# A two-layer decoder trunk on one core: first transfers on two queues, the last block in one half, tiles in multiples of 64 bytes

## The chip, the core and the metric

The kernel runs on one core of a Trainium2 chip. The core has a matrix engine (TensorE, PE in the profile; its weight loads are listed apart as PEld), a vector engine (VectorE, DVE), an engine for functions of single elements (ScalarE, ACT), GpSimd (POOL) and SyncE (SP), and 16 DMA engines that move data between memory (HBM) and the core's on-chip memory (SBUF). A transfer is issued by SP or by ACT and goes into that issuer's queue. TensorE writes its sums into PSUM, from which VectorE and ScalarE read them.

The metric is the device time of one execution in microseconds. Three runs of the kernel before took 2359.57 to 2361.82 us, median 2360.89.

## The reference

The input x has 256 tokens of 2048 features, in float32. Two layers follow one another; each is a mixer and a gated MLP, both with a root-mean-square norm before them and the input added after them.

```python
for l in range(DEPTH):                      # DEPTH = 2
    h = rms_norm(x, mix_norm[l])
    if l % 2 == 0:
        h = mixer_ab(h, ...)                # one input projection, gated MLP over tokens and
                                            # a gated linear recurrence, one output projection
    else:
        h = mixer_c(h, ...)                 # attention with a forget gate, 16 heads of 128
    x = x + h
    h = rms_norm(x, ffn_norm[l])
    x = x + conv_ffn(h, ...)                # up (2048 -> 2 x 5632), conv of width 3, silu gate, down
return x
```

Nearly all of the arithmetic is products of 256 tokens with weight matrices in float32, about 430 MB of weights in all, each read once.

## The kernel before

All arrays are laid out feature-major: a tile has 128 features on the partitions and 256 tokens in a row. x stays in SBUF as 16 such tiles (xT), in seven buffers of 1, 1, 2, 2, 2, 4 and 4 tiles (x0, x1, x2, x4, x6, x8, x12 by their first tile). Each float32 number is split into a high part, rounded to the type that TensorE multiplies in one pass (fp32r), and the rest, the low part. A product is formed as high x high + high x low + low x high.

For weights this is done by `weights` (L130): a transfer into w by SP (L137), the high part wh by ScalarE (L139), the low part wl by VectorE (L141). There are four buffers for w and three each for wh and wl. For inputs it is done by `split` (L199), with the norm's gain multiplied in: high part by ScalarE (L204), low part by VectorE (L205); `feed_split` (L230) applies it to one tile of x, and the result, tile a, holds high and low part side by side, 2 x 256 columns. The norm's factor per token is applied after the product.

`project` (L144) makes one block of 128 output features: for each of 16 feature tiles one matmul of 512 columns (wh against both parts of a, L155) and one of 256 (wl against the high part, added to the second half, L158). Its result has two halves, which `fold` (L187) or `add_x` (L262) adds: ScalarE copies the second half to SBUF (L265), VectorE adds the first half to x (L266) and then the copy (L267). `project_tok` (L163) makes 512 output features for all tokens at once, with the tokens' parts as the weights that are loaded into TensorE: per feature tile two halves of the tokens with three matmuls of 512 columns each (L180 to L182).

The first work of the kernel is `project_tok` on w_v with feed=True. Its loop takes one feature tile at a time for the first four and two at a time after that; before each step it issues the x transfers that FETCH lists for that k, calls feed_split for its tiles, lets one step of waiting side work run (`tick`), and calls weights. Transfers of x tiles from 8 on are issued by ACT, the others by SP, ahead of the weights of the same step. Fifteen matmuls on a tile of ones (warm) run before. The order in which each engine gets its instructions is fixed by a scheduler when the program is built; an engine works through its list in that order and waits where a tile isn't ready. A transfer signals on one of a few semaphores, in turn; one that gets a semaphore still in use waits until the earlier transfer has landed.

The side work in the first blocks is the sum of squares for the norm (`feed_square`, L237 to L241). At the end of the second MLP, `down` computes the last four blocks with project, and `finish_x` stores each x tile as it is done.

Tiles are given SBUF addresses one behind the other in pools, in steps of 32 bytes. Several tiles are only 1, 2, 24 or a few columns wide, so the tiles behind them stand at addresses that are a multiple of 32 but not of 64.

Of the kernel before, what the change touches and what calls it, by code (L numbers as in the profile page):

```python
# [14 lines left out]
P = 128  # L15
# [9 lines left out]
WARM = 15  # L25
FETCH = {0: (0,), 1: (1, 2, 8), 2: (4, 6), 3: (12,)}
# [19 lines left out]
def tile_trunk(ctx: ExitStack, tc: tile.TileContext, x, pp_d, cst_d, mlev_d, msk_d,  # L46
# [13 lines left out]
    def nm(base):  # L60
        count[0] += 1
        return f"{base}_{count[0]}"
# [13 lines left out]
    nc.sync.dma_start(pp[:, 0:C_FFN], pp_d[:, 0:C_FFN])  # L76
# [53 lines left out]
    def weights(src, n, rows=None):  # L130
# [5 lines left out]
        w = pool.tile([P, n], F32, tag="w", name=nm("w"), bufs=nw)  # L136
        nc.sync.dma_start(w if rows is None else w.rearrange("p (m c) -> p m c", m=rows), src)  # L137
        wh = pool.tile([P, n], F32R, tag="wh", name=nm("wh"), bufs=ns)
        SC.activation(wh, w, AF.Copy)  # L139
        wl = pool.tile([P, n], F32R, tag="wl", name=nm("wl"), bufs=ns)  # L140
        V.tensor_tensor(wl, w, wh.bitcast(F32), ALU.subtract)  # L141
        return wh, wl

    def project(wsrc, acts, chunks=(8, 8), k0=0, run=2):  # L144
        ps = pm.tile([P, 512], F32, tag="pm", name=nm("pm"))
        nk = sum(chunks)
        done = 0
        for c in chunks:
            lo = (k0 + done) * P
            tick()  # L150
            wh, wl = weights(wsrc[:, lo:lo + c * P], c * P)
            for k1 in range(0, c, run):
                ks = range(k1, min(k1 + run, c))
                for k in ks:
                    PE.matmul(ps, wh[:, k * P:(k + 1) * P], acts[done + k],  # L155
                              start=done + k == 0, stop=False, skip_group_check=True)
                for k in ks:
                    PE.matmul(ps[:, S:2 * S], wl[:, k * P:(k + 1) * P], acts[done + k][:, 0:S],  # L158
                              start=False, stop=done + k == nk - 1, skip_group_check=True)
            done += c  # L160
        return ps

    def project_tok(wsrc, norm, feed=False):  # L163
        ps = [pm.tile([P, 512], F32, tag="pm", name=nm("pm")) for _ in range(2)]
        k = 0
        for c in ((1, 1, 1, 1) + (2,) * 6 if feed else (2,) * 8):
            if feed:
                for c0 in FETCH.get(k, ()):
                    t, c0, n = fetch[c0]
                    (SC if c0 >= 8 else nc.sync).dma_start(t, x[:, c0:c0 + n, :])  # L170
                for i in range(c):
                    norm.feed_split(k + i)
            tick()
            wh, wl = weights(wsrc[:, k * 512:(k + c) * 512], c * 512)
            for T in range(2):
                for i in range(c):
                    a = norm.a[k + i]
                    ah, al = a[:, T * P:(T + 1) * P], a[:, S + T * P:S + (T + 1) * P]
                    h, l = (t[:, i * 512:(i + 1) * 512] for t in (wh, wl))
                    PE.matmul(ps[T], ah, h, start=k + i == 0, stop=False)  # L180
                    PE.matmul(ps[T], ah, l, start=False, stop=False)  # L181
# [17 lines left out]
    def split(dst, src, gain=None):  # L199
# [3 lines left out]
        else:  # L203
            SC.activation(dst[:, 0:S], src, AF.Copy, scale=gain)  # L204
# [3 lines left out]
    def rsq(dst, src, n):  # L208
        tag = "sq" if dst.shape[-1] == S else f"rm{len(dst.shape)}{dst.shape[-1]}"
        m = tp.tile(list(dst.shape), F32, tag=tag, name=nm("rm"))  # L210
        t = tp.tile(list(dst.shape), F32, tag=tag, name=nm("rt"))
# [11 lines left out]
    class Norm:  # L223
# [6 lines left out]
        def feed_split(self, k):  # L230
            a = apool.tile([P, 512], F32R, tag="a", name=nm("a"), bufs=KT)
            split(a, xT[k], pp[:, self.col + k:self.col + k + 1])
            self.a[k] = a
# [14 lines left out]
        def finish(self, tok=False):  # L248
# [10 lines left out]
            Rt = cp.tile([P, 2], F32, tag="Rt", name=nm("Rt"), bufs=2)  # L259
# [10 lines left out]
    def mixer_ab(norm):  # L270
# [90 lines left out]
        ge = hp.tile([P, 3 * NH], F32, tag="ge", name="ge")  # L361
# [32 lines left out]
        def hgrn(h):  # L394
# [15 lines left out]
            for li in reversed(range(NL)):  # L410
# [8 lines left out]
                if li:  # L419
                    V.tensor_tensor(odd, odd, view(tot, m, (-m, 2), (2, m // 2), (0, n)), ALU.mult)  # L420
                    nt = hp.tile([P, m], F32, tag=f"tot{n}", name=nm("tot"), bufs=1)
# [34 lines left out]
            so = hp.tile([P, 2], F32, tag="so", name=nm("so"), bufs=2)  # L456
# [74 lines left out]
    def mixer_c(norm):  # L531
# [9 lines left out]
        gq = hp.tile([P, 1], F32, tag="gq", name="gq")  # L541
# [23 lines left out]
        def attend(h, q, k, v):  # L565
# [20 lines left out]
            mxs = hp.tile([P, 2], F32, tag="mxs", name=nm("mxs"), bufs=2)  # L586
            sms = hp.tile([P, 2], F32, tag="sms", name=nm("sms"), bufs=2)
# [62 lines left out]
    def ffn(l, norm, last):  # L650
# [52 lines left out]
        def down(g, hid):  # L703
            final = g == HT // GRP - 1
            late = []
            for q in range(4):
                if final and q == 3:
                    for m in range(4 * q, KT):
                        ps = project(w_dn[l, m], hid, chunks=(6, 5), k0=g * GRP, run=2)
# [3 lines left out]
                        add_x(m, ps)  # L713
# [124 lines left out]
```

## Time and profile before

| | |
|---|---|
| median of three runs | 2360.89 us (2359.57 to 2361.82) |
| the profiled execution | 2359.05 us |
| its span, first to last instruction | 2357.2 us |
| granted TensorE clock, mean over the span | 1.000 |
| moved by DMA | 439.56 MB, 186 GB/s over the span |

The page gives the busy time of each engine and its share of the span, then the chain of work that ended last, followed back from the last instruction. Groups and timelines have lines of the form: start and length, engine, line of the kernel, operation, tiles written and read, shapes, count; in brackets stands how long the engine was idle before, and what ended that. Windows give the busy time of each engine (with its number of instructions), the granted clock, the DMA engines' share and GB/s for a stretch of time. DMA issues stand with the time from issue to landing. SPq and ACTq are the queues' issuing instructions. Matmuls overlap, so a row's length is longer than the distance to the next one's start.

### The profile page before, as it was taken

The numbers are of one execution on the slowest core, as the hardware profiler recorded it, in microseconds if no ns is written. First come the engines' busy times: TensorE is split into PE (matmuls) and PEld (weight loads), VectorE is DVE, ScalarE is ACT, GpSimd is POOL, SyncE is SP. The second block draws the span as 40 slices with busy tenths as digits, with TensorE's granted clock in tenths as the row PEclk, the third lists the DMA queues.
The fourth block names the chain that finished last, engine by engine and source line by source line (L and its number), as shares of the span: only waits on it lengthen the run. The fifth ranks groups of instructions, "written<-read, shape, count | busy, mean of one in ns | idle before, by whom it ended". The sixth has DMA issues, their size and how long they took to land.

```text
span 2357.2 us, 33532 instructions
## 1 busy us (share of the span) xinstructions
PE 2348.7 (100%) x12528; PEld 2011.1 (85%) x12528; DVE 1689.0 (72%) x2760; ACT 1286.3 (55%) x2085; POOL 0.2 (0%) x4
## 2 busy tenths in 40 slices
PE   9999999999999999999999999999999999999999
PEld 7888888888888888888888888888888888888887
DVE  7777877878847757866766666777878757758755
ACT  7655665655545545544555455556555545545533
POOL 0000000000000000000000000000000000000000
PEclk9999999999999999999999999999999999999999
DMA  7544455655555565555655554556555565565563
GB/s 269 179 166 150 150 197 206 222 188 188 179 196 196 184 192 197 184 181 164 202 171 180 171 161 169 188 188 239 190 190 189 179 203 190 179 202 191 178 193 117
DMA packets 194740, 439.56 MB, mean 186 GB/s; under 512 B 14208, under 2 KB 108688, under 8 KB 194448
## 3 DMA queue, kind: packets, MB, share of 16 engines
q1 hardware_dynamic: 193424, 434.20, 55.3%
q10 hardware_dynamic: 1152, 3.21, 0.4%
q8 instruction: 98, 1.61, 0.3%
q14 instruction: 66, 0.54, 0.1%
HBM read 435.24 MB, written 2.11 MB: 186 GB/s over the span
## 4 chain that ended last, share of the span: by engine, by line
PE 99%; DMA 0%; ACT 0%; DVE 0%; SPq 0%; issue 0%; ACTq 0%
PE pm L155 42%; PE pm L158 21%; PE pm L728 6%; PE pm L727 6%; PE pm L729 6%; PE pm L181 5%; PE pm L182 5%; PE pm L180 5%; PE px L432 1%; DMA w<-in_w_v 0%; PE px L606 0%; PE px L692 0%; PE px L570 0%; PE px L577 0%; PE px L601 0%; PE px L402 0%
## 5 line engine op out<-in xcount | busy, mean ns | idle before, releaser
L141 DVE TENSOR_TENSOR wl<-w,wh 128x1024 fp32r<-128x1024 f32 (+1 forms) x840 | 1004.3, 1196 | 556.2 <-ACT wh L139 553.9
L139 ACT ACTIVATE wh<-w 128x1024 fp32r<-128x1024 f32 (+1 forms) x840 | 871.1, 1038 | 962.2 <-PE pm L155 473.1
L155 PE MATMUL pm<-a,wh 128*128 128x512 f32 x3600 | 1135.3, 396 | 0.0
L158 PEld LDWEIGHTS pm<-a,wl 128*128 128x128 f32 x3600 | 676.1, 188 | 158.9
L158 PE MATMUL pm<-a,wl 128*128 128x256 f32 x3600 | 708.7, 278 | 0.0
L155 PEld LDWEIGHTS pm<-a,wh 128*128 128x128 f32 x3600 | 549.6, 189 | 1.5 <-DVE a L205 0.8
L727 PE MATMUL pm<-wh,hid 128*128 128x512 f32 x660 | 257.1, 390 | 0.0
L728 PE MATMUL pm<-wl,hid 128*128 128x512 f32 x660 | 256.8, 389 | 0.0
L729 PE MATMUL pm<-wh,hid 128*128 128x512 f32 x660 | 256.8, 389 | 0.0
L180 PE MATMUL pm<-wh,a 128*128 128x512 f32 x512 | 203.1, 398 | 2.6 <-ACT wh L139 2.6
L181 PE MATMUL pm<-wl,a 128*128 128x512 f32 x512 | 200.8, 392 | 0.6 <-DVE wl L141 0.6
L182 PE MATMUL pm<-wh,a 128*128 128x512 f32 x512 | 200.2, 391 | 0.0
L729 PEld LDWEIGHTS pm<-wh,hid 128*128 128x128 f32 x660 | 123.9, 188 | 25.7
L727 PEld LDWEIGHTS pm<-wh,hid 128*128 128x128 f32 x660 | 123.9, 188 | 25.5
L728 PEld LDWEIGHTS pm<-wl,hid 128*128 128x128 f32 x660 | 123.9, 188 | 25.3
L180 PEld LDWEIGHTS pm<-wh,a 128*128 128x128 f32 x512 | 96.2, 188 | 22.4 <-ACT wh L139 3.7
L181 PEld LDWEIGHTS pm<-wl,a 128*128 128x128 f32 x512 | 96.2, 188 | 21.3 <-DVE wl L141 2.2
L182 PEld LDWEIGHTS pm<-wh,a 128*128 128x128 f32 x512 | 96.1, 188 | 19.8
L667 ACT ACTIVATE conv<-ev,pp 128x256 f32<-128x256 f32 x176 | 102.9, 585 | 5.5 <-DVE ev L196 5.5
L189 DVE TENSOR_TENSOR ev<-pm,ev 128x256 f32<-128x256 f32 x225 | 93.9, 417 | 1.1 <-ACT ev L188 1.0
L669 DVE SCALAR_TENSOR_TENSOR conv<-ev,pp,conv 128x254 f32<-128x254 f32 x176 | 85.0, 483 | 6.2
L668 DVE SCALAR_TENSOR_TENSOR conv<-ev,pp,conv 128x255 f32<-128x255 f32 x176 | 84.1, 478 | 4.4 <-ACT conv L667 4.4
(185 smaller groups left out, 1644.3 us busy)
## 6 DMA issues: line engine op xcount, KB each, us to landing
w<-in_w_up SPq DMA_DIRECT2D x352, 512.0 KB, 4.2
w<-in_w_dn SPq DMA_DIRECT2D x150, 512.0 KB, 3.6
w<-in_w_cqkv SPq DMA_DIRECT2D x96, 512.0 KB, 3.5
w<-in_w_abo SPq DMA_DIRECT2D x32, 512.0 KB, 3.6
w<-in_w_cg SPq DMA_DIRECT2D x32, 512.0 KB, 3.6
w<-in_w_co SPq DMA_DIRECT2D x32, 512.0 KB, 3.6
w<-in_w_f SPq DMA_DIRECT2D x16, 512.0 KB, 3.7
w<-in_w_q SPq DMA_DIRECT2D x16, 512.0 KB, 3.6
```

The costliest lines, as they stand in the source:

```text
L139: SC.activation(wh, w, AF.Copy)
L141: V.tensor_tensor(wl, w, wh.bitcast(F32), ALU.subtract)
L155: PE.matmul(ps, wh[:, k * P:(k + 1) * P], acts[done + k], start=done + k == 0, stop=False, skip_group_check=True)
L158: PE.matmul(ps[:, S:2 * S], wl[:, k * P:(k + 1) * P], acts[done + k][:, 0:S], start=False, stop=done + k == nk - 1, skip_group_check=True)
L180: PE.matmul(ps[T], ah, h, start=k + i == 0, stop=False)
L181: PE.matmul(ps[T], ah, l, start=False, stop=False)
L182: PE.matmul(ps[T], al, h, start=False, stop=k + i == KT - 1)
L189: V.tensor_tensor(t, ps[:, 0:S], t, ALU.add)
L667: SC.activation(c, z, AF.Identity, bias=pp[:, cb:cb + 1], scale=w(2))
L727: PE.matmul(ps[T], ah, h, start=k + i == 0, stop=False)
L728: PE.matmul(ps[T], ah, lo_, start=False, stop=False)
L729: PE.matmul(ps[T], al, h, start=False, stop=k + i == GRP - 1)
```

## The change

Three things are changed.

The start: the first weights (256 KB) are issued by SP before anything else, the first five x buffers (x0 to x6) by ACT, in front of ScalarE's table load, and pp's first columns by SP after the weights. x8 and x12 are issued by SP, behind the weights of the steps k=4 and k=8 (an ordering without a wait keeps them there). The high part of the first x tile is made by VectorE. In the single-tile steps the six matmuls run with wh first, both halves and both parts, and then wl. There are 11 warm-up matmuls in place of 15.

The end: the last block is summed in one half of 256 columns with three matmuls of 256 columns per feature tile, and one VectorE addition to x replaces the copy and two additions.

The tiles: those that were 4 to 96 bytes wide, and pp (3216 bytes, now 3264), are rounded up to a multiple of 64 bytes (LANE is 16 numbers of 4 bytes), and only their first columns are used. The two helper tiles in `rsq` share one tag and size.

The core of the diff; the lines left out give the other small tiles (ge, tot, so, gq, mxs, sms) the same rounding as one1 and Rt:

```diff
-WARM = 15
-FETCH = {0: (0,), 1: (1, 2, 8), 2: (4, 6), 3: (12,)}
+WARM = 11
+FETCH = {4: (8,), 8: (12,)}
+LANE = 16
...
-    pp = cp.tile([P, NPP], F32, tag="pp", name="pp")
+    pp = cp.tile([P, -(-NPP // LANE) * LANE], F32, tag="pp", name="pp")
...
-    one1 = cp.tile([P, 1], F32, tag="one1", name="one1")
-
+    one1 = cp.tile([P, LANE], F32, tag="one1", name="one1")[:, 0:1]
+
+    first = wp.tile([P, 512], F32, tag="w", name=nm("w"), bufs=4)
+    nc.sync.dma_start(first, w_v[0, :, 0:512])
+    for t, c0, n in xload[:5]:
+        SC.dma_start(t, x[:, c0:c0 + n, :])
     nc.sync.dma_start(pp[:, 0:C_FFN], pp_d[:, 0:C_FFN])
...
+        if w is None:
+            w = pool.tile([P, n], F32, tag="w", name=nm("w"), bufs=nw)
+            deep["dma"] = nc.sync.dma_start(
+                w if rows is None else w.rearrange("p (m c) -> p m c", m=rows), src)
...
+                if narrow:
+                    for k in ks:
+                        for j, t in enumerate((wh, wh, wl)):
+                            o = S if j == 1 else 0
+                            PE.matmul(ps[:, 0:S], t[:, k * P:(k + 1) * P], acts[done + k][:, o:o + S],
+                                      start=done + k + j == 0, stop=j == 2 and done + k == nk - 1)
+                    continue
...
+            later = []
             if feed:
                 for c0 in FETCH.get(k, ()):
                     t, c0, n = fetch[c0]
-                    (SC if c0 >= 8 else nc.sync).dma_start(t, x[:, c0:c0 + n, :])
+                    later.append((t, c0, n))
                 for i in range(c):
-                    norm.feed_split(k + i)
+                    norm.feed_split(k + i, V if k == 0 else SC)
             tick()
-            wh, wl = weights(wsrc[:, k * 512:(k + c) * 512], c * 512)
+            wh, wl = weights(wsrc[:, k * 512:(k + c) * 512], c * 512, w=first if feed and k == 0 else None)
+            for t, c0, n in later:
+                r = nc.sync.dma_start(t, x[:, c0:c0 + n, :])
+                tc.add_manual_dep(r.ins, deep["dma"].ins.name, order, reason="queue order")
+            if feed and c == 1:
+                a = norm.a[k]
+                for j, (o, t) in enumerate(((0, wh), (S, wh), (0, wl))):
+                    for T in range(2):
+                        PE.matmul(ps[T], a[:, o + T * P:o + (T + 1) * P], t, start=k + j == 0, stop=False)
+                k += c
+                continue
...
-            Rt = cp.tile([P, 2], F32, tag="Rt", name=nm("Rt"), bufs=2)
+            Rt = cp.tile([P, LANE], F32, tag="Rt", name=nm("Rt"), bufs=2)[:, 0:2]
...
-                        ps = project(w_dn[l, m], hid, chunks=(6, 5), k0=g * GRP, run=2)
+                        ps = project(w_dn[l, m], hid, chunks=(6, 5), k0=g * GRP, run=2,
+                                     narrow=last and m == KT - 1)
...
-                        add_x(m, ps)
+                        if last and m == KT - 1:
+                            V.tensor_tensor(xT[m], xT[m], ps[:, 0:S], ALU.add)
+                        else:
+                            add_x(m, ps)
```

More of the change, by code (lines that the diff above doesn't have):

```diff
@@ L1 @@
+import math
 from contextlib import ExitStack
@@ L128, in tile_trunk, with weights @@
     deep = {"pool": None, "turn": 0}
-    def weights(src, n, rows=None):
+    def weights(src, n, rows=None, w=None):
         deep["turn"] += 1
@@ L209, in rsq @@
         tag = "sq" if dst.shape[-1] == S else f"rm{len(dst.shape)}{dst.shape[-1]}"
-        m = tp.tile(list(dst.shape), F32, tag=tag, name=nm("rm"))
-        t = tp.tile(list(dst.shape), F32, tag=tag, name=nm("rt"))
+        cols = dst.shape[-1] if dst.shape[-1] == S else LANE // math.prod(dst.shape[1:-1])
+        m, t = (tp.tile(list(dst.shape[:-1]) + [max(cols, dst.shape[-1])], F32, tag=tag, name=nm(n_))
+                [..., 0:dst.shape[-1]] for n_ in ("rm", "rt"))
         V.tensor_scalar(m, src, 1.0 / n, EPS, ALU.mult, ALU.add)
```

27 lines of the change are left out of this document (14 added, 13 removed).

## The prediction

> **What bounds the kernel.** The page's busy times and its chain of waits come first: is there one engine that everything waits for, and where does it not run?
>
> ```profile
> span 2357.2 us, 33532 instructions
> PE 2348.7 (100%) x12528; PEld 2011.1 (85%) x12528; DVE 1689.0 (72%) x2760; ACT 1286.3 (55%) x2085; POOL 0.2 (0%) x4
> PE 99%; DMA 0%; ACT 0%; DVE 0%; SPq 0%; issue 0%; ACTq 0%
> ```
>
> TensorE carries 99% of the chain, so only three things move the end: how long it idles before its stream closes up, the pace of the stream, and what follows its last matmul. Weight traffic, ScalarE and VectorE are covered by it everywhere else, and the change leaves all that order as it was from the second block of projections on. The timeline of the start:
>
> ```profile
> 0.72 1.28 ACT L119 ACT_TABLE_LOAD   x1 [0.72 <-PEq L827]
> 0.73 0.39 SPq L76 DMA_DIRECT2D pp<-in_pp  x1
> 0.76 0.39 ACTq L170 DMA_DIRECT2D x<-in_x  x1
> 1.04 5.10 PE L122 MATMUL warm<-ones 128*128 128x128 f32 x30 [1.04 <-DVE one L78]
> 1.17 0.42 SPq L170 DMA_DIRECT2D x<-in_x  x1
> 1.64 0.42 SPq L137 DMA_DIRECT2D w<-in_w_v  x1
> 5.72 0.51 ACT L204 ACTIVATE a<-x,pp 128x256 fp32r<-128x256 f32 x1 [3.72 <-DMA x<-in_x]
> 6.82 0.63 ACT L139 ACTIVATE wh<-w 128x512 fp32r<-128x512 f32 x1 [0.59 <-DMA w<-in_w_v]
> 7.50 0.73 PE L180 MATMUL pm<-wh,a 128*128 128x512 f32 x2 [1.36 <-ACT wh L139]
> ...
> 12.20 1.39 ACT L139 ACTIVATE wh<-w 128x512 fp32r<-128x512 f32 x2 [0.40 <-DMA w<-in_w_v]
> 13.49 1.29 ACT L204 ACTIVATE a<-x,pp 128x256 fp32r<-128x256 f32 x3
> 14.69 1.04 ACT L139 ACTIVATE wh<-w 128x1024 fp32r<-128x1024 f32 x1
> 15.64 0.90 ACT L204 ACTIVATE a<-x,pp 128x256 fp32r<-128x256 f32 x2
> 15.77 1.23 DVE L141 TENSOR_TENSOR wl<-w,wh 128x1024 fp32r<-128x1024 f32 x1 [0.27 <-ACT wh L139]
> 17.05 0.50 PE L181 MATMUL pm<-wl,a 128*128 128x512 f32 x1 [0.40 <-DVE wl L141]
> 21.03 0.40 ACT L237 ACTIVATE acc<-x 128x256 f32<-128x256 f32 x1
> 21.34 0.71 ACT L240 ACTIVATE sq<-x 128x256 f32<-128x256 f32 x2
> ```
>
> The first projection waits in turn for x, for the weights, for ScalarE's high part (wh) and for VectorE's low part (wl). From 17.05 us it runs without a gap, as the windows show:
>
> ```profile
> 2.00:4.00 2.00, 2.00 (x12) 2.00 (x11) 0.00 (x0) 0.01 (x1) 0.00 (x0) 1.00 0.85 275
> 8.00:11.00 3.00, 2.61 (x9) 1.43 (x9) 1.99 (x6) 2.08 (x5) 0.00 (x0) 1.00 1.01 387
> 17.05:33.00 15.95, 15.95 (x70) 13.21 (x71) 14.04 (x27) 13.53 (x24) 0.00 (x0) 1.00 0.85 281
> ```
>
> The columns after the length are PE, PEld, DVE, ACT, POOL, granted clock, DMA share and GB/s. The first block has 8 pairs of 12 matmuls, 96; 70 of them lie in the last row, 15.95 / 70 = 0.228 us each, so 26 were done at 17.05. A stream without any gap that ends at the same moment would have begun at 17.05 - 26 x 0.227 = 11.15 us. I call that the virtual start; only what the change does to this number counts at the start.
>
> **Part 1, the start.** The change issues the first weights (256 KB) first on SP, x0, x1 and x2-7 on ACT's queue beside them, puts x8-11 and x12-15 on SP behind the weights of k=4 and k=8, and computes the first high part of x on VectorE. The first x tile and weights no longer stand behind pp, x8-11 (512 KB, at 0.76) and each other. The issues, with their times to landing from 0 to 30 us:
>
> ```profile
> x<-in_x ACTq DMA_DIRECT2D x2, 512.0 KB, 5.3
> w<-in_w_v SPq DMA_DIRECT2D x4, 256.0 KB, 5.5
> x<-in_x SPq DMA_DIRECT2D x2, 128.0 KB, 4.8
> pp<-in_pp SPq DMA_DIRECT2D x1, 16.0 KB, 2.9
> ```
>
> x0 is now the first of its queue, as pp was, so 2.9 us is its lower bound and 4.8 its upper; I take 2.9, because pp too had one larger transfer beside it. x0 then lands at 0.76 + 2.9 = 3.7 us. A wait is added: the fifth x transfer (x6-7) reuses x0's semaphore, so it stands on ACT until x0 has landed, and the table load and the first wh are queued behind it; TensorE waits for that wh. So wh starts at 3.7 + 0.35 (an issue; the rows have 0.39) + 1.28 (table) = 5.35 us, where it started at 6.82. With 4.8 it would be 7.2 and nothing would be won there. VectorE makes the high part of x meanwhile, once pp, second on SP, has landed; its cover is 1.65 us of ScalarE.
>
> From there ScalarE sets the pace. In its new order, up to the weights of k=6,7, stand 4 wh of 512 columns at 0.645 (12.20 to 13.49 for two), 11 high parts of x at 0.43 (13.49 to 14.69 for three is 0.40 each, the pair at 15.64 0.45), one wh of 1024 at 0.95 (14.69 to 15.64), two squares at 0.31 and 0.35, a second wh at 1.04, and then, 0.05 us later, VectorE's wl at 1.23: 2.58 + 4.73 + 0.95 + 0.66 + 1.04 + 0.05 + 1.23 = 11.2 us. At that moment 38 matmuls can be done, 8.6 us of stream, and the 10 that are left, 2.3 us, cover the two squares, the wh and the wl of the next weights. The virtual start is 5.35 + 11.2 - 8.6 = 7.95 us, if the data are in time. The fourth weights are the tight ones: with them 4 x 256 KB of weights, 1 MB of x and pp must have landed, 2.1 MB. At the 275 to 387 GB/s of the rows from 1.7 us on that is 7.2 to 9.4 us; ScalarE asks for them after three wh and three high parts of x, at 5.35 + 1.94 + 1.29 = 8.6. I take 9.0, near the slow end since the queues start at the slow rate, so 0.4 us late: virtual start 8.35, gain 11.15 - 8.35 = **2.8 us** (bounds 0.9, with x0 after 4.8 us, and 3.2, with no late weights). Later weights (issued when VectorE frees a buffer at about 6.7) and x8-11 have 0.5 us or more to spare. Eleven warm-up matmuls for fifteen (5.10 us) end at about 4.8 us, before the first wh in either case, and the pause after them, 1.2 us to 6.0, is no longer than the 1.36 of now, in which the granted clock stayed at 1.00: nothing; should the pause cost clock, the stream still waits for ScalarE until 17 us.
>
> The page "DMA: Bandwidth & Descriptors" of the Trainium skill, under "Issuing engines are not separate DMA queues", says that transfers started from several engines run on the same 16 DMA engines and that a second issuer only saves the issuing time. The trace agrees so far as two queues together never pass 387 GB/s above. By that rule the second queue brings no bytes sooner, and what is won is the order alone; where the first four weights would be no earlier, rival C has the time.
>
> **Part 2, alignment.** Tiles of 4, 8 or 96 bytes per partition become multiples of 64, so what lies behind them moves from an odd multiple of 32 to a multiple of 64. Weight tiles, a, hid and yc were on 64 before and stay there. On TensorE's large matmuls that leaves the inputs ya and yb of the output projection of mixer AB, on 32 until now. The trace holds a pair for comparison: the same loop, the same 512 matmuls, once with ya and yb and once in mixer C with yc.
>
> ```profile
> 311.36:401.89 90.53, 90.53 (x514) 78.68 (x512) 63.58 (x97) 50.95 (x82) 0.00 (x0) 1.00 0.53 187
> 1529.23:1618.57 89.34, 89.34 (x514) 77.64 (x512) 62.83 (x96) 51.21 (x82) 0.00 (x0) 1.00 0.54 189
> ```
>
> The difference, 90.53 - 89.34 = **1.2 us**, is what the alignment is worth if it is the cause; the lower bound is 0, the upper 1.2 plus what the small matmuls give (rival E). The other tiles moved are read and written by VectorE and ScalarE, which the 99% covers.
>
> The page "SBUF — State Buffer" of the Trainium skill (its box on cachelines, under "Door 1: The DMA port swizzle") gives 16-byte lines. An offset of 32 bytes is a whole number of those, so by it the alignment would change nothing; the row of 90.53 speaks against it, not proof, and rival B has that case.
>
> **Part 3, the end.** The last block is summed in one 256-column half, so the copy of the second half and its addition go.
>
> ```profile
> 2349.29 0.62 PE L155 MATMUL pm<-hid,wh 128*128 128x512 f32 x2
> ...
> 2352.54 0.40 PE L158 MATMUL pm<-hid,wl 128*128 128x256 f32 x2
> ...
> 2353.00 0.28 PE L158 MATMUL pm<-hid,wl 128*128 128x256 f32 x1
> 2353.37 0.38 ACT L265 ACTIVATE ev<-pm 128x256 f32<-128x256 f32 x1 [3.50 <-PE pm L158]
> 2353.78 0.42 DVE L266 TENSOR_TENSOR x<-x,pm 128x256 f32<-128x256 f32 x1 [3.00 <-ACT ev L265]
> 2354.24 0.42 DVE L267 TENSOR_TENSOR x<-x,ev 128x256 f32<-128x256 f32 x1
> ```
>
> One addition can start at 2353.37 and end at 2353.79 instead of 2354.66: 0.87 us. On TensorE 11 matmuls of 512 and 11 of 256 columns become 33 of 256. The old ones took 2353.00 + 0.12 - 2349.29 = 3.83 us, the new ones 33 x 0.115 to 0.12 (0.40 - 0.28 between the starts of a pair) = 3.8 to 3.96; I take 0.05 dearer. Gain **0.8 us** (0.7 to 0.9). The store behind it keeps its 2.5 us to the end of the span.
>
> **The sum.** 2.8 + 1.2 + 0.8 = 4.8 us. The profiled execution took 2359.05 us (span 2357.2 and 1.85 around it), which becomes 2354.25. The median of the three runs is 1.84 us above it, so the forecast is 2360.89 - 4.8 = **2356.1 us**, 0.20% less, about at the edge of what a measurement of this kernel tells from no change (0.2%, 4.7 us).
>
> **Rivals.**
> A is the forecast. With its start anywhere from 2.0 to 3.2 and the end from 0.7 to 0.9 us it gives 2355.6 to 2357.0.
> B: the start and the end hold, the alignment brings nothing; 1.2 us less won, 2357.3. For it speaks that the two output projections sit in different stages with other work on VectorE (63.58 against 62.83 us); against it, that ScalarE was busier in the quicker one.
> C: the queues only share what there is. x2-7 on ACT take half of the DMA engines and the fourth weights land as late as before (ScalarE's 12.20 row shows the third and fourth landing about then), or x0 lands at 4.8 us. The start then gains 0 to 0.9, the sum is 2.0 to 2.9, 2358 to 2358.9.
> D, on the other side: new addresses slow the stream. All weights and inputs get other addresses, those of the first pools 128 bytes further on, and TensorE reads the two operands side by side. 4.8 / 12528 = 0.38 ns a matmul cancels the gain; 1 ns more each gives 2360.89 + 12.5 - 4.8 = 2368.6. Against it: weights and inputs in different buffers show one duration (a and yc),
>
> ```profile
> L155 PE MATMUL pm<-a,wh 128*128 128x512 f32 x3600 | 1135.3, 396 | 0.0
> L155 PE MATMUL pm<-yc,wh 128*128 128x512 f32 x256 | 80.5, 396 | 0.0
> L432 PE MATMUL px<-E 128*128 128x128 f32 x112 | 15.5, 279 | 0.0
> L692 PE MATMUL px<-cst,y 128*128 128x128 f32 x64 | 8.0, 272 | 0.0
> ```
>
> and the distance between weights and inputs in the first pools stays the same.
> E: alignment also helps the small matmuls, whose inputs E, pt, qk, kq and st stand on 32. E's take 279 ns, those of the aligned y 272, 2.5%; the windows give all matmuls into px 91.11 us,
>
> ```profile
> 0.00:2357.20 2357.20, 91.11 (x582) 76.57 (x582) 53.92 (x136) 33.02 (x106) 1.00 0.56 186
> ```
>
> so at most 2.3 us more, and with the aligned ones left out I take 1.6: 2354.5.
>
> **Chances.** A 0.58, of which six tenths lie beyond 4.7 us: its sum is just there, and the 0.4 us for late weights may not be owed; E 0.16; C 0.11; B 0.09; D 0.06. Faster by over 0.2%: 0.35 + 0.16 = 0.51; within: 0.23 + 0.20 = 0.43; slower 0.06. The range leaves D and the ends out: 2353.4 (E with an ideal start and a run of the spread shown, 1 us) to 2359.2 (C at its worst). A's own is 2355.6 to 2357.0.
>
> **What will show it.** The timeline: first wh at 5.35 us, first matmul of the projection at 6.0, no gap from 17.0 on with 38 done (virtual start 8.35). The window of the first output projection: 89.3 instead of 90.5. The tail: no ScalarE copy after the last matmul, one VectorE addition. The forecast is wrong if x0 lands late and holds the table load, if ScalarE waits more than 1 us for the third or fourth weights, if the 90.5 stays, or if matmuls start further apart than 0.227 us in the long stages.

## The result, and the profile after

The changed kernel is slower. Its median is 2366.97 us (2366.30 to 2367.23, nine runs) beside 2360.89 us of the kernel before (nine runs), a ratio of 1.0024 with the 95% interval 1.0016 to 1.0033. One of the nine runs of the kernel before took 3916.09 us and is left out of the ratio. The forecast was 2356.1 us, with a range up to 2359.2. The profiled execution took 2367.14 us, its span is 2365.3 us, 8.1 us more than before.

The page after, busy times and chain of waits:

```profile
span 2365.3 us, 33538 instructions
PE 2358.9 (100%) x12531; PEld 2015.6 (85%) x12531; DVE 1688.9 (71%) x2760; ACT 1286.2 (54%) x2083; POOL 0.2 (0%) x4
PE 99%; DMA 0%; ACT 0%; DVE 0%; issue 0%; ACTq 0%; SPq 0%
```

The bound is the same: TensorE has 99% of the chain, and nobody waits for a new thing. Yet TensorE is busy 10.2 us longer with three matmuls more. The matmuls themselves are further apart. The groups of matmuls say where; first those of the kernel before (L158 is the 256-column matmul of `project`, L727 to L729 are the down projection of the MLP), then those of the kernel after, in the same form:

```profile
L158 PE MATMUL pm<-a,wl 128*128 128x256 f32 x3600 | 708.7, 278 | 0.0
...
L727 PE MATMUL pm<-wh,hid 128*128 128x512 f32 x660 | 257.1, 390 | 0.0
L728 PE MATMUL pm<-wl,hid 128*128 128x512 f32 x660 | 256.8, 389 | 0.0
L729 PE MATMUL pm<-wh,hid 128*128 128x512 f32 x660 | 256.8, 389 | 0.0
```

```profile
L170 PE MATMUL pm<-a,wh 128*128 128x512 f32 x3600 | 1135.4, 396 | 0.0
...
L173 PE MATMUL pm<-a,wl 128*128 128x256 f32 x3600 | 714.5, 280 | 0.0
...
L761 PE MATMUL pm<-wh,hid 128*128 128x512 f32 x660 | 259.0, 392 | 0.0
L763 PE MATMUL pm<-wh,hid 128*128 128x512 f32 x660 | 258.9, 392 | 0.0
L762 PE MATMUL pm<-wl,hid 128*128 128x512 f32 x660 | 258.7, 392 | 0.0
```

The 512-column matmuls with a (L170) are as they were. The 256-column ones with a carry 5.8 us more, those of the down projection 5.9 us more, with the same instructions and counts. Nothing in the diff touches either. Windows over stretches in which TensorE never stops show the same as plain lengths. First before, then after; the columns after the length are busy time and count of PE, PEld, DVE, ACT and POOL, granted clock, DMA share, GB/s. The first row of each is the second group of 22 up projections in layer 0, the second row a piece of the down projection of 366 matmuls:

```profile
707.77:830.37 122.60, 122.60 (x705) 106.98 (x704) 96.64 (x149) 69.51 (x109) 0.00 (x0) 1.00 0.56 188
1012.82:1095.80 82.98, 82.98 (x368) 68.68 (x367) 45.60 (x50) 35.20 (x38) 0.00 (x0) 1.00 0.63 189
```

```profile
706.44:829.77 123.33, 123.33 (x705) 107.58 (x704) 96.67 (x149) 69.53 (x109) 0.00 (x0) 1.00 0.57 187
1013.84:1098.03 84.19, 84.19 (x369) 68.66 (x367) 45.57 (x50) 35.22 (x38) 0.00 (x0) 1.00 0.62 187
309.02:398.34 89.32, 89.32 (x513) 77.62 (x512) 63.46 (x97) 51.03 (x82) 0.00 (x0) 1.00 0.56 189
1531.96:1621.33 89.37, 89.37 (x513) 77.90 (x512) 62.84 (x96) 51.21 (x82) 0.00 (x0) 1.00 0.57 189
```

PE is busy through every one of them, at a granted clock of 1.00: neither a wait nor the clock, but the pace. A group of up projections is 0.73 us longer and there are 8, 5.8 us; the stretches of the down projection (5 in each layer, 1980 matmuls with high and low parts) add up to 455.9 us where they had 449.3, 6.6 us. The last two rows are the output projections of mixer AB, which won its 1.2 us (90.53 before), and of mixer C, unchanged (89.34).

The start, from the timeline after (the part on which the forecast speaks):

```profile
0.74 3.93 ACTq L81 DMA_DIRECT2D x<-in_x  x5
...
4.70 1.28 ACT L125 ACT_TABLE_LOAD   x1 [4.70 <-DMA x<-in_x]
...
5.99 0.63 ACT L147 ACTIVATE wh<-w 128x512 fp32r<-128x512 f32 x1
...
7.59 0.63 ACT L147 ACTIVATE wh<-w 128x512 fp32r<-128x512 f32 x1 [0.57 <-DMA w<-in_w_v]
...
8.90 0.63 ACT L147 ACTIVATE wh<-w 128x512 fp32r<-128x512 f32 x1 [0.28 <-DMA w<-in_w_v]
...
17.62 0.50 PE L207 MATMUL pm<-wl,a 128*128 128x512 f32 x1 [0.25 <-DVE wl L149]
```

The last gap of the stream ends at 17.62 us, with 38 matmuls done: a virtual start of 17.62 - 38 x 0.227 = 9.0 us. The first block's 96 matmuls are through at 30.91 us instead of 33.07, 2.2 us won. The end:

```profile
2358.20 0.40 PE L166 MATMUL pm<-hid,wh 128*128 128x256 f32 x2
...
2362.01 0.28 PE L166 MATMUL pm<-hid,wl 128*128 128x256 f32 x1
2362.33 0.42 DVE L745 TENSOR_TENSOR x<-x,pm 128x256 f32<-128x256 f32 x1 [2.63 <-PE pm L166]
```

After the last matmul's start stand 0.74 us (2362.01 to 2362.75) instead of 1.66 (2353.00 to 2354.66); the 33 small matmuls take 3.93 us instead of 3.83: 0.8 us won. The account closes: +5.8 + 6.6 for the slower matmuls, -2.2, -1.2 and -0.8 for the rest, +8.2 us, where the spans differ by 8.1.

### The profile page after: what moved, and what is told of

The parts are those of the page before. It is cut to its first block, busy times and chain, and to the rows that moved or that the text cites. A ratio compares the mean times of both kernels' runs of the same rounds, so it can differ in the third digit from the quotient of the medians.

```text
span 2365.3 us, 33538 instructions
## 1 busy us (share of the span) xinstructions
PE 2358.9 (100%) x12531; PEld 2015.6 (85%) x12531; DVE 1688.9 (71%) x2760; ACT 1286.2 (54%) x2083; POOL 0.2 (0%) x4
## 4 chain that ended last, share of the span: by engine, by line
PE 99%; DMA 0%; ACT 0%; DVE 0%; issue 0%; ACTq 0%; SPq 0%
PE pm L170 41%; PE pm L173 21%; PE pm L763 6%; PE pm L762 6%; PE pm L761 6%; PE pm L207 5%; PE pm L208 5%; PE pm L206 5%; PE px L462 1%; DMA x<-in_x 0%; PE px L636 0%; PE px L722 0%; PE px L600 0%; PE px L607 0%; PE px L631 0%; PE pm L166 0%
## 5 line engine op out<-in xcount | busy, mean ns | idle before, releaser
L170 PE MATMUL pm<-a,wh 128*128 128x512 f32 x3600 | 1135.4, 396 | 0.0
L173 PEld LDWEIGHTS pm<-a,wl 128*128 128x128 f32 x3600 | 676.6, 188 | 159.7
L173 PE MATMUL pm<-a,wl 128*128 128x256 f32 x3600 | 714.5, 280 | 0.0
L170 PEld LDWEIGHTS pm<-a,wh 128*128 128x128 f32 x3600 | 551.3, 189 | 1.6 <-DVE a L234 0.8
L206 PE MATMUL pm<-wh,a 128*128 128x512 f32 x504 | 199.9, 397 | 0.4 <-ACT wh L147 0.4
L208 PE MATMUL pm<-wh,a 128*128 128x512 f32 x504 | 196.9, 391 | 0.0
```

Of the source, the lines that this page charges most:

```text
L170: PE.matmul(ps, wh[:, k * P:(k + 1) * P], acts[done + k], start=done + k == 0, stop=False, skip_group_check=True)
```

## The experiments

**What the matmuls' operands have in common.** What changed for them can only be where their operands stand. The addresses that the build gives, in bytes on a partition modulo 256 (all weight tiles are multiples of 256 long, so one number holds for all buffers of a set):

```
                                            before  after
first weight buffers, and a (both in the
  pools opened first)                          128      0
second weight buffers, and hid (MLP's pools)   128    128
yc (mixer C's pool)                            128    128
ya, yb (mixer AB's pool)                       224      0
```

The first pools moved by 128 bytes, the MLP's by 256: in between lies the pool with the two helper tiles of `rsq`, and their rounding adds another 128 bytes. Before, a, hid, yc and both sets of weights were a multiple of 256 apart from one another; after, the first weights and a stand 128 from hid and the second weights. The slow matmuls are those that pair the two groups: 256-column matmuls of a with the second weights (L173), and the down projection's of hid with the first weights. That made the theory: **the distance modulo 256 between the operand that streams and the one that is loaded sets the pace.** (The profile names the streaming operand first: in `project` a streams and a weight tile is loaded, in the down projection wh or wl streams and hid is loaded.) The rivals: something else in the change (start or end) slows the stream; the absolute address of hid does; the 128 bytes cost nothing and the helper tiles' own size does.

Where a start-to-start time is given below, it is the mean over the trace's starts of the consecutive pairs of such matmuls (1190 for a with the second weights, 810 for hid with the first); the few pairs that stand over 300 ns apart are left out (4 of the 810).

**1. The distance restored, all of the change kept.** An idle tile of 128 bytes at the head of the MLP's and of mixer C's pool; the computation is the same, here and in all the runs with idle tiles.

```diff
+        nc.gpsimd.memset(hp.tile([P, 32], F32, tag="pad", name=nm("pad")), 0.0)
```

> The changed kernel with one idle tile of 128 bytes per partition at the head of the MLP's and of mixer C's pool, so that the tiles of these two pools move by 128 bytes; nothing else differs. Theory R (a matmul slows when the address of its moving operand and that of the weight tile loaded beside it differ by something that is no multiple of 256 bytes; the change made that difference 128 in the MLP and in mixer C's output projection): the difference is a multiple of 256 again, the long stages return to their old pace, some 10 to 12 us go, 2355 to 2357 us. Theory S (the new start order or something in its wake costs the time): 2367 as the changed kernel. Theory A (the alignment to 64 bytes as such is harmful): 2367, since all tiles stay on multiples of 64.

Measured: 2354.40 us (2353.80 to 2355.25) against 2359.67, ratio 0.9976 (0.9967 to 0.9985). The two stretches are back to the lengths before:

```profile
703.40:826.00 122.60, 122.60 (x705) 106.98 (x704) 96.65 (x149) 69.59 (x109) 0.00 (x0) 1.00 0.58 188
1008.45:1091.43 82.98, 82.98 (x368) 68.67 (x367) 45.59 (x50) 35.21 (x38) 0.00 (x0) 1.00 0.63 189
```

Beside the kernel before, the change stands at +6.1 us without and at -5.3 us with the 128 idle bytes: they are worth 11.4 us, and this version beats both kernels.

**2. The distance spoiled in the kernel before.** The same line in the MLP's pool of the kernel before, and nothing else.

> The kernel before with the same idle tile of 128 bytes in the MLP's pool alone: hid and the second set of weight buffers move by 128 bytes against the first set and against a. Theory R: the MLP's matmuls slow as in the changed kernel, 9 to 11 us more than before, 2370 to 2372. Theories S and A: 2361, no change.

Measured: 2371.62 us (2371.13 to 2373.91), ratio 1.0052 (1.0039 to 1.0064), 12 us slower without any of the change. The stretches:

```profile
710.03:833.37 123.34, 123.34 (x706) 107.58 (x704) 96.67 (x149) 69.57 (x109) 0.00 (x0) 1.00 0.56 187
1017.44:1101.62 84.18, 84.18 (x368) 68.65 (x367) 45.57 (x50) 35.21 (x38) 0.00 (x0) 1.00 0.61 187
```

They are the changed kernel's to 0.01 us. So the loss in these stretches needs neither the new start nor the new end.

**3. Only the helper tiles of `rsq` undone.**

```diff
-        cols = dst.shape[-1] if dst.shape[-1] == S else LANE // math.prod(dst.shape[1:-1])
-        m, t = (tp.tile(list(dst.shape[:-1]) + [max(cols, dst.shape[-1])], F32, tag=tag, name=nm(n_))
-                [..., 0:dst.shape[-1]] for n_ in ("rm", "rt"))
+        m = tp.tile(list(dst.shape), F32, tag=tag, name=nm("rm"))
+        t = tp.tile(list(dst.shape), F32, tag=tag, name=nm("rt"))
```

> The changed kernel with the two helper tiles of rsq in their old, unrounded sizes; one part undone. This takes 128 bytes out in front of the later pools, so hid, yc and the second weight buffers stand a multiple of 256 from the first weights again, but ya and yb are now 128 off. Theory R: MLP and mixer C's output projection back at their old pace (about 11 us less than the changed kernel), the output projection of mixer AB slower than in the changed kernel by about 1 us: 2356 to 2358. Theories S and A: 2367.

Measured: 2354.64 us (2354.00 to 2356.00), ratio 0.9979 (0.9970 to 0.9988). The rounding of these two tiles makes the whole loss, and run 1 says that it does so by what it moves, since there they keep their new size. A miss within it: ya and yb now stand 128 off the weights, and their output projection was expected to lose 1 us, but didn't:

```profile
703.91:826.52 122.61, 122.61 (x706) 106.98 (x704) 96.66 (x149) 69.55 (x109) 0.00 (x0) 1.00 0.57 188
1008.97:1091.95 82.98, 82.98 (x369) 68.65 (x368) 45.59 (x50) 35.20 (x38) 0.00 (x0) 1.00 0.63 189
308.70:398.07 89.37, 89.37 (x514) 77.92 (x512) 63.44 (x97) 50.99 (x82) 0.00 (x0) 1.00 0.56 189
```

There the 256-column matmuls are 117.4 ns apart instead of 115.2, and the 512-column ones 231.2 instead of 233.1, which cancels. The changed kernel shows the same with yc (117.5 and 231.2). So the cost of 128 bytes is not the same in every sequence of matmuls.

**4. The start alone, in the kernel before.** WARM, FETCH, the first transfers and the new order in `project_tok` and `feed_split`, with every tile as before and the old end.

> The kernel before with the new start alone (transfers, first high part on VectorE, order of the single steps, 11 warm-ups), tiles and end as before. Theory R: the start is worth what the trace of the changed kernel shows there, about 2.2 us less, 2358.7. Theory S: 2366 or more.

Measured: 2356.89 us (2356.04 to 2357.63), 2.8 us less than 2359.67, ratio 0.9986 (0.9978 to 0.9995). In its trace the first 96 matmuls are through at 30.96 us, 2.1 us earlier than before. The start's gain is there; the output projection of AB keeps its old length, since its tiles do:

```profile
309.15:399.68 90.53, 90.53 (x513) 78.69 (x512) 63.55 (x97) 50.98 (x82) 0.00 (x0) 1.00 0.55 187
```

**5 and 6. 256 and 384 bytes instead of 128, in the kernel before.** With 256, hid and the second weights get the very addresses of the changed kernel (modulo 2048) but keep their distance to the first pools modulo 256. With 384 the distance is 128 again, to the other side.

```diff
+        nc.gpsimd.memset(hp.tile([P, 64], F32, tag="pad", name=nm("pad")), 0.0)
```

> The kernel before with an idle tile of 256 bytes in the MLP's pool: hid and the second weight buffers get the same addresses modulo 2048 (1408) that they have in the changed kernel, but against the first buffers they are moved by 256, twice what slowed it. Theory R (only the distance between the two operands counts, in steps of 256 or 512): no change, 2360. A theory of absolute addresses (tiles on 1408 are slow): 10 us more, 2370.

> The kernel before with 384 bytes in the MLP's pool. The distance from a to the second weight buffers is then 384 modulo 512 instead of the slow 128. Theory R in its first form (any distance that is no multiple of 256 is slow): 2370. Theory R with a sign (128 modulo 512 is slow, 384 is not, as the output projections of the changed kernel and of the run with the old rsq tiles suggest, where 384 cost nothing): 2360.

Measured: with 256 bytes 2359.43 us against 2359.89, ratio 0.9999 (0.9990 to 1.0009): nothing. With 384 bytes 2371.95, ratio 1.0051 (1.0038 to 1.0065): all of the loss. The 366 matmuls of the down projection, 256 bytes in the first fence and 384 in the second:

```profile
1012.56:1095.53 82.97, 82.97 (x368) 68.67 (x367) 45.61 (x50) 35.21 (x38) 0.00 (x0) 1.00 0.63 189
```

```profile
1017.34:1101.53 84.19, 84.19 (x369) 68.66 (x368) 45.58 (x50) 35.21 (x38) 0.00 (x0) 1.00 0.64 187
```

The rival of the absolute address falls with the first, and with the second the thought that the sign of the distance matters. Start-to-start times over these runs: hid with the first weights 226.7 to 226.8 ns at a distance of 0 or 256 (before, runs 1, 3 and 5) and 232.8 to 232.9 at 128 or 384 (after, runs 2 and 6); a with the second weights in 256 columns 115.1 to 115.6 and 119.3. Run 1 has hid and the first weights both at 0 (modulo 256) where the kernel before has both at 128, and 226.8 ns is the time of both: here too the address by itself does nothing. Hid with the second weights, whose distance is 0 in all of these runs, has 226.7 to 226.8 ns where the first ones stand well and 228.1 to 228.2 where they don't: a part of the loss spills over to neighbours, in a way that these runs don't explain.

**7. The pace by itself.** This kernel leaves the whole model out: it has rows of 64 equal matmuls, one row for each distance, and beside them only the filling of the two operand tiles at its start and a store at its end. It ran once.

```diff
+    for i in range(64):
+        PE.matmul(ps[i % 2][:, 0:512], sta[:, 32:32 + P], mov[:, 0:512], start=True, stop=True)
```

> A kernel that leaves the whole computation out and only repeats matmuls of one weight tile and one moving tile, 64 per line: the weight tile moved by 0 to 512 bytes in steps of 32 against the moving one (256 columns), then both together by 32 to 256, then 512 columns, then the moving tile alone. Output is zeros and sums of no meaning. Theory R: 113 to 115 ns at distance 0 and 256, 117 to 125 at distances in between, and no difference when both are moved together. An absolute theory: the lines with both moved differ from distance 0.

The rows for 512 columns, with the weight tile moved by 0, 32, 64, 128, 256, 384 and 512 bytes in the order of their lines (L111, 113, 115, 117, 119, 121, 123), as the groups view has them:

```profile
L115 PE MATMUL pm<-mov,sta 128*128 128x512 f32 x64 | 15.1, 395 | 0.0
L113 PE MATMUL pm<-mov,sta 128*128 128x512 f32 x64 | 15.1, 395 | 0.0
L121 PE MATMUL pm<-mov,sta 128*128 128x512 f32 x64 | 15.0, 395 | 0.0
L117 PE MATMUL pm<-mov,sta 128*128 128x512 f32 x64 | 15.0, 395 | 0.0
L111 PE MATMUL pm<-mov,sta 128*128 128x512 f32 x64 | 14.7, 390 | 0.0
L119 PE MATMUL pm<-mov,sta 128*128 128x512 f32 x64 | 14.7, 389 | 0.0
L123 PE MATMUL pm<-mov,sta 128*128 128x512 f32 x64 | 14.7, 389 | 0.0
```

Start to start, past the first eight pairs of a row: 226.7 ns at 0, 256 and 512, and 232.2 to 233.4 at all the others. That is nearly the down projection's pair of numbers, without VectorE, ScalarE or weight traffic beside it: the effect needs no other engine's work, and it has the period 256. In 256 columns the period is the same while the weight tile is the one that moves, and the order is not: 120.0 ns at 0, 160 and 256 bytes, 118.4 at 32, 117.3 at 96, 118.7 at 128, 116.7 at 224, though the kernel's 256-column matmuls are slower off the multiple. Moving both operands together leaves 120.0 in each of four rows.

Four more rows move the streaming tile alone, by 32, 64, 128 and 256 bytes. Three of them have the time of the same distance modulo 256 (116.7, 118.7 and 120.0 ns). The fourth hasn't: with the streaming tile moved by 64 (L127) the starts are 113.3 ns apart, with the weight tile moved by 192 (L81), the same distance modulo 256, 117.8.

```profile
L81 PE MATMUL pm<-mov,sta 128*128 128x256 f32 x64 | 7.7, 279 | 0.0
...
L127 PE MATMUL pm<-mov,sta 128*128 128x256 f32 x64 | 7.4, 276 | 0.0
```

So at 512 columns the distance gives the pace; at 256 columns the distance modulo 256 is not the whole rule, and a single row of equal matmuls doesn't give the 256-column numbers of the kernel, where two differing loads and lengths alternate. That part of the expectation was missed.

**8. The table load ahead of the x transfers, on top of run 1.** What held the first wh was ScalarE's table load behind the fifth x transfer.

```diff
+    SC.preload_act_table_set(LNEXP)
...
-    SC.preload_act_table_set(LNEXP)
```

> The changed kernel with the 128-byte tiles of the first run and ScalarE's table load issued ahead of the x transfers, so that it no longer stands behind x0's landing. If the first wh is held by the table load: wh starts about 1 us earlier (5.0 us), and the total is 0.3 to 1 us below the first run's, 2353.5 to 2354. If the weights' landing holds the steps after it anyway: no change, 2354.4.

Measured: 2354.62 us against run 1's 2354.40: no gain. The first wh starts at 4.73 us (6.16 in run 1), but the next wait is for the second weights:

```profile
4.73 0.63 ACT L147 ACTIVATE wh<-w 128x512 fp32r<-128x512 f32 x1 [2.72 <-DMA pp<-in_pp]
...
6.96 0.63 ACT L147 ACTIVATE wh<-w 128x512 fp32r<-128x512 f32 x1 [1.20 <-DMA w<-in_w_v]
```

The first matmul starts at 5.76 us where run 1 had 6.84, and 96 are through at 29.75 where run 1 had 30.21: of 1.1 us 0.5 are left. What is late next is the landing of the weights.

**9. Mixer AB's pool moved, in the kernel before.** An idle tile of 160 bytes at its head. All of this pool's tiles move with it; of these the matmuls of the output projection read ya and yb alone.

```diff
+        nc.gpsimd.memset(hp.tile([P, 40], F32, tag="pad", name=nm("pad")), 0.0)
```

> The kernel before with one idle tile of 160 bytes at the head of mixer A and B's pool and nothing else, so that ya and yb stand a multiple of 256 bytes from the first weight buffers (1024 instead of 1184). The computation is unchanged. The distance theory: the output projection of mixers A and B takes 89.3 us from its first to its last matmul instead of 90.53 (the 256-column starts 115.2 ns apart instead of 121.2, the 512-column ones 233.4 instead of 232.3), the MLP and the rest stay as before (226.9 ns, 115.4 ns), and the whole falls by 1.2 us, to about 2358.6 against 2359.9. The rival, that the gain in that stage of the changed kernel came from another of the rounded tiles or from the earlier start: the stage stays at 90.5 and the whole within 0.3 us of the kernel before.

Measured: 2358.20 us against 2359.27, 1.1 us less, ratio 0.9995 (0.9986 to 1.0004), too little to tell by times alone; the stage tells it:

```profile
311.48:400.81 89.33, 89.33 (x514) 77.63 (x512) 63.48 (x97) 51.01 (x82) 0.00 (x0) 1.00 0.56 189
```

So the 1.2 us of this stage come from where the pool's tiles stand, with their sizes, the start and the end as before; that it is ya and yb among them follows from what the stage's matmuls read and was not tested apart.

**10. All roundings, neither the new start nor the new end.** The tile part of the diff in the kernel before.

> The kernel before with all of the rounded tiles and neither the new start nor the new end: the addresses of the changed kernel, the order of the kernel before. The distance theory: the MLP's down projections at 233.0 ns per matmul instead of 226.9, the 256-column matmuls with the second set of weight buffers at 119.3 instead of 115.4 (as in the changed kernel), the output projection of A and B at 89.3 us; altogether +12 and -1.2, so 2370 to 2371.5 where the kernel before has 2359.9. The sum rule (start -2.8 us as measured alone, end -0.8): the changed kernel's 2367.0 plus 3.6 gives 2370.6. The rival, that start or end themselves cost something beside the roundings: then this run stays clearly under 2370.

Measured: 2370.01 us (2369.77 to 2371.20) against 2359.27, ratio 1.0045 (1.0031 to 1.0059), 10.7 us slower:

```profile
708.89:832.23 123.34, 123.34 (x706) 107.60 (x704) 96.67 (x149) 69.54 (x109) 0.00 (x0) 1.00 0.58 187
1016.30:1100.49 84.19, 84.19 (x369) 68.65 (x368) 45.57 (x50) 35.22 (x38) 0.00 (x0) 1.00 0.63 187
311.45:400.80 89.35, 89.35 (x514) 77.65 (x513) 63.51 (x97) 51.02 (x82) 0.00 (x0) 1.00 0.57 190
```

All three effects of the tiles in one run, and the parts add up: 10.7 for the tiles, less 2.8 for the start (run 4) and 0.8 for the end, is 7.1; the changed kernel's median is 6.1 us above that of before, in runs that differ by 1 to 2 us among themselves.

**11. The low halves wl 64 bytes further, on top of run 1.** Two idle tiles in the first weight buffers' pool: wl now stands 64 (modulo 256) from a and from hid, and wh and all of the second buffers keep their multiples.

```diff
         wh = pool.tile([P, n], F32R, tag="wh", name=nm("wh"), bufs=ns)
         SC.activation(wh, w, AF.Copy)
+        if deep["turn"] == 1:
+            nc.gpsimd.memset(wp.tile([P, 48], F32, tag="pad1", name=nm("pad"), bufs=1), 0.0)
         wl = pool.tile([P, n], F32R, tag="wl", name=nm("wl"), bufs=ns)
+        if deep["turn"] == 1:
+            nc.gpsimd.memset(wp.tile([P, 16], F32, tag="pad2", name=nm("pad"), bufs=1), 0.0)
```

> The changed kernel with the 128-byte idle tile of the earlier run (2354.4 us) and two more idle tiles in the first weight buffers' pool, so that the low halves wl stand 64 bytes (mod 256) from the normalised inputs a, while the high halves wh and the second set of buffers keep their multiples of 256. The computation is unchanged. Form one of the theory, the pace depends on the operand that streams and the weight tile that is loaded beside it: where a 512-column matmul with wh is followed by a load of wl, and in the matmuls of queries, keys and values whose moving operand is wl, the start-to-start times change by up to 6 ns, and a 256-column matmul with wl that is followed by a load of wh keeps its time; form two, the matmul's own two operands: the 256-column matmuls with wl change throughout, also where wh is loaded next. By the repeated matmuls a 256-column matmul at 64 bytes would be 6 ns faster (113.3 against 119.8); by the projections at 128 bytes 4 ns slower (119.3 against 115.4). With about 2030 such matmuls and 500 moving wl: 2349 to 2364 us in all; the likeliest is slower than 2354.4 by 2 to 8 us.

Measured: 2358.70 us (2358.43 to 2360.31), ratio 0.9999 (0.9990 to 1.0008), where run 1 has 2354.40. The three stretches:

```profile
703.57:825.89 122.32, 122.32 (x706) 107.10 (x704) 96.67 (x149) 69.69 (x109) 0.00 (x0) 1.00 0.58 188
1008.87:1092.98 84.11, 84.11 (x369) 68.65 (x367) 45.61 (x50) 35.22 (x38) 0.00 (x0) 1.00 0.63 187
308.60:397.52 88.92, 88.91 (x514) 77.72 (x512) 63.55 (x97) 51.12 (x82) 0.00 (x0) 1.00 0.57 190
```

In the projections form one (the operand that streams and the tile loaded beside it, for the next matmul) holds better than form two (a matmul's own two operands): a 512-column matmul with wh goes from 233.3 to 229.0 ns where a wl at 64 is loaded next, a 256-column one with wl from 114.7 to 117.2 where another wl follows, and one where a wh follows keeps its time (116.2 and 115.8). Form two asked for a change there too. The changed kernel has a second test, where its matmuls pass from one set of weights to the other: a 256-column matmul of a whose own weights stand at 0 and the next ones at 128 takes 123.2 ns, one with its own at 128 and the next at 0 takes 116.7; with all at multiples of 256 (before, runs 1 and 3) both have 112.5 to 115.8. So the next load weighs most, though not alone. The net in run 11 is a gain in the projections: a group of up projections is 0.28 us shorter, the output projection 0.4. In the down projection everything got slower, 226.7 to 229.8 ns even with the second buffers, whose distances were all left at multiples of 256. Neither form explains that.

## Why the prediction was wrong, step by step

**The bound** was read rightly: TensorE's stream, and three things that can move its end. The step that failed is the second of these, its pace, where Part 2 says that weight tiles, a, hid and yc "were on 64 before and stay there" and goes on to ya and yb alone. Each stayed on 64, but they did not stay where they were to one another. The sum holds the pace at nothing; it measured 12.4 us (5.8 in the up projections, 6.6 in the down projection). The prediction's own last sign of being wrong is the one that came: in the down projection with the first weights, matmuls start 232.9 ns apart and not 227.

**Rival D** is what happened, at a price close to its own example: 12.4 us over 12531 matmuls is 0.99 ns each. It got 0.06, for two reasons that don't hold. "Weights and inputs in different buffers show one duration" was true because before every such pair (a, hid and yc with both sets of weights) stood at a multiple of 256; the rows held no other distance, so they could say nothing of one. They were also rows of `project`'s 512-column matmuls, which keep their time even at a distance of 128 (with a and the second weights 233.1 ns start to start before, 233.0 after). The only pair that stood otherwise was ya and yb with the weights, at 160, and that was the stage with the unexplained 1.2 us. Its 256-column rows showed two durations in the profile before:

```profile
L158 PE MATMUL pm<-yc,wl 128*128 128x256 f32 x256 | 50.2, 278 | 0.0
...
L158 PE MATMUL pm<-ya,wl 128*128 128x256 f32 x128 | 25.8, 284 | 0.0
```

The second reason, that "the distance between weights and inputs in the first pools stays the same", is right for the first pools and says nothing of the matmuls that cross from the first pools to the later ones: the down projection with the first weights, and a with the second. The diff shows the step: the `rsq` tiles get longer, and their pool lies between. Runs 2, 3 and 10 settle that it is this one, runs 1, 5 and 6 that in these sequences the distance and not the address counts. By what mechanism the distance slows TensorE, no run shows.

**Part 1**, the start, was right in mechanism and too large: 2.2 us in the profiled execution where 2.8 was forecast. The term that was off is x0's landing. Its two bounds were 2.9 and 4.8 us and 2.9 was taken; in the trace after, transfers of 128 KB at the start take 3.5 us at the median, and the table load, queued behind that wait as forecast, starts at 4.70 instead of 4.05. So the first wh starts at 5.99 instead of 5.35. From there to the closing of the stream it takes 11.6 us, as worked out (11.2 + 0.4), but in part by luck: ScalarE waited 0.85 us and not 0.4, for the second and third weights (0.57 and 0.28 us) and not the fourth, and its own work was as much shorter. The warm-up matmuls took 5.02 us and ended at 6.06 us instead of 4.8, which cost nothing: the first wh was ready later still, and the projection's first matmul came at 6.67. From execution to execution it varies: run 1, with the same start, has 96 matmuls through at 30.21 us, 2.9 us earlier than before.

**Part 2**, its gain of 1.2 us at ya and yb, came to the last digit (89.32 us), and run 9 shows that it comes from where the tiles stand. That it needs a multiple of 64, or of 256 from the weights, isn't told apart: at distances of 0, 64 for wl alone, and 128 (runs 9, 11 and 3) the stage takes 89.33, 88.92 and 89.37 us, and all three are multiples of 64.

**Part 3**, the end, came as forecast, 0.8 us.

**The other rivals.** B had it that the alignment brings nothing: refuted by run 9. C had part of the truth about x0. E had the small matmuls gain from alignment; the windows give all matmuls into px 91.05 us after, 91.11 before, so they gain next to nothing:

```profile
0.00:2365.30 2365.30, 91.05 (x582) 76.51 (x582) 53.94 (x136) 33.08 (x106) 1.00 0.58 186
```

With the distance mended (run 1) the sum of the forecast comes out, near enough: 2359.67 - 2354.40 = 5.3 us less, where 4.8 was worked out.

## What to carry to other kernels

When a change alters the size of any tile, list which large tiles behind it move and by how much against each other; an argument that each one keeps its alignment isn't enough where one engine reads two at once. A row that shows one duration for many operand pairs is evidence only for the distances that occur among them, so look for the one pair that stands differently, and take its unexplained time seriously. A loss that shows as longer groups with the same counts, no idle time and a granted clock of 1.00 is a matter of pace: compare the windows of one stage before and after, and undo the placement, not the work.

## What the runs showed of the hardware that was not expected

- The pace of back-to-back matmuls depends on the distance between the operand that streams and the one that is loaded: in rows of equal matmuls of 512 columns it is 226.7 ns at a multiple of 256 bytes, 232.2 to 233.4 at the other distances tried (32, 64, 128 and 384 bytes). Moving both operands together changes nothing (120.0 ns in four rows of 256 columns). At 256 columns the multiple is among the slowest (120.0 ns, as at 160 bytes), and one row (113.3 ns, where 117.8 has the same distance modulo 256) fits no rule by the distance modulo 256 alone.
- In the kernel a distance of 128 bytes is worth 12 us of 2360 in the MLP and nothing net in the output projections, where 256 and 512 columns alternate (89.37 us at 128, 89.33 at 0). At 64 bytes for one of the two weight halves the projections are even faster (122.32 us instead of 122.60 for a group). Which rule covers the sequences with two lengths, and why run 11's down projection slowed with the untouched buffers too, stays open.
- An idle tile is free: with 256 bytes of it the time is the same (ratio 0.9999).
